# Where the second rounding of weights is kept: out of PSUM in one half of up, into PSUM in the early projection

## The chip, the cores and the metric

The kernel runs on one core of a Trainium2 chip. The metric is device time in microseconds (us): the median of three runs. One more execution was profiled; its trace gives the rows below.

## The reference

One layer of a streaming encoder on 512 tokens of width 2048, in float32. A vector c conditions it: `mod = silu(c) @ ada_w + ada_b` gives six rows of 2048 (shift, scale and gate of the mixing half, and of the FFN half).

```
h = rms_norm(x, mix_pre_g) * (1 + sc_m) + sh_m
y = token_mixers(h, w_in, ...)          # one input projection, four mixers, one output projection
x = x + gt_m * rms_norm(y, mix_post_g)
h = rms_norm(x, ffn_pre_g) * (1 + sc_f) + sh_f
a, gt = split(h @ w_up)                 # 2048 x 11008
a = causal_dwconv(a, conv_w) + conv_b   # 3 taps along time
y = (gelu(a) * gt) @ w_down             # 5504 x 2048
x = x + gt_f * rms_norm(y, ffn_post_g)
```

## The kernel before

Every large product is made from two fp32r numbers per operand. `hi` is the operand rounded by a ScalarE copy, `lo` is the rest, made by VectorE as operand minus `hi`, and three matmuls (hi x hi, lo x hi, hi x lo) are summed in PSUM. So each 128 x 512 piece of weights costs a ScalarE copy and a VectorE subtraction. `split` does this for the projections, `dsplit` for the FFN. With `shadow`, `dsplit` makes the rounding twice, once into SBUF (`hi`, for the matmuls) and once into a PSUM bank (`sh`), and VectorE subtracts `sh`. A list, `SHADOW = (0, 1, 2, 3)`, says in which steps of a block.

PSUM has eight banks here: four of the tag `acc` and four of the tag `mx`. Shadows, transposes and small results all take theirs from `mx`.

*Early projection.* The 16 k tiles of h are finished one after another, since each needs its part of `mod`: a matrix-vector product (`gemv_unit`), of which VectorE and GpSimd each sum a half of the units (ScalarE scales GpSimd's half), `join` adds the two, and a matmul with ones turns the row into columns (`mod_cols`, or `first_half` for the first two tiles). Meanwhile the projection columns that are needed first go through the k tiles that exist, in six steps (`KSTEPS`: four of two k tiles, two of four). `fm_group` and `tm_group` make their weights with `wunit`; partial sums are added in SBUF by `ev_early_fm` (L586) and `ev_early_tm` (L598). `x_norm` makes the row of 1/rms of x (`rB`): ScalarE squares 16 tiles, VectorE adds them up.

*Up and down.* `fast_block` makes a block of products with seven steps (`STEPS`) instead of eight; in each step, for each of four weight pieces, two output tiles get three matmuls each. GpSimd makes the differences of weights that the later steps use (L1461, L1464, L1466, L1468; each after the `lo` of the piece that it overwrites). Up runs 20 blocks, ten in each of two halves `p`. In the second half each block's results are complete: its eight 512-column tiles are transposed (`cT`, 32 transposes, two `mx` banks for each of four feature tiles) and go through `glu`: ScalarE, VectorE twice, ScalarE, VectorE once. GpSimd sums the results for down (`put_sums`). Then the next block follows. Down runs ten blocks with the same `fast_block`.

The order of the instructions on each engine is not written out: a planner takes the program's order as priority and what it expects to be ready.

Of the kernel before, what the change touches and what calls it, by code (L numbers as in the profile page):

```python
# [11 lines left out]
F32R = mybir.dt.float32r  # L12
AF = mybir.ActivationFunctionType
# [236 lines left out]
def trunk_kernel(ctx: ExitStack, tc: tile.TileContext, a: dict, out: bass.AP):  # L250
# [33 lines left out]
    def tt_(s="t"):  # L284
        return tp.tile([P, 512], F32, tag="t", name=nm(s))
# [53 lines left out]
        return r, sd  # L339


    def wunit(src, nk, w, own=True):

        raw = wraw() if own else araw()
        nc.sync.dma_start(out=raw[:, :nk * w], in_=src[:, :nk * w])
        step = max(1, 512 // w)
        out_ = []
        for j in range(0, nk, step):
            m = min(step, nk - j) * w
            hi = wp.tile([P, 512], F32R, tag="hi", name=nm("hi"))  # L350
            lo = wp.tile([P, 512], F32R, tag="lo", name=nm("lo"))
            split(raw[:, j * w:j * w + m], hi[:, :m], lo[:, :m])
            out_ += [(hi[:, i * w:(i + 1) * w], lo[:, i * w:(i + 1) * w]) for i in range(min(step, nk - j))]
        return out_

# [3 lines left out]
    def araw():  # L359
        return gp.tile([P, UW], F32, tag="ada", name=nm("ada"), bufs=NADA)  # L360

    def split(src, hi, lo, eng=None):
        S.activation(hi, src, AF.Copy)  # L363
        (eng or V).tensor_tensor(lo, src, hi, ALU.subtract)  # L364

# [29 lines left out]
            return gp.tile([P, 512], dt, tag="ga", name=nm(s), bufs=NGA)  # L395
        return mt(s, dt=dt)

    def gemv_unit(accs, eng, uidx, i, half=None):
        w = 512 if half is None else 256
        if half is None:  # L400
            raw = araw()
            nc.sync.dma_start(out=raw, in_=a["ada"][uidx])
        else:
            raw = mt("ada")
            nc.sync.dma_start(out=v2(raw), in_=v2(a["ada"][uidx])[:, :, half * 256:(half + 1) * 256])
        for j in range(2):
            c1 = cond[:, 2 * i + j:2 * i + j + 1]
            src = raw[:, j * w:(j + 1) * w]
            if eng not in accs:
                accs[eng] = galloc("ga")[:, :w]  # L410
                if eng is V:
                    V.tensor_scalar(accs[eng], src, c1, None, ALU.mult)
                else:
                    S.activation(accs[eng], src, AF.Copy, scale=c1)
            elif eng is V:
                V.scalar_tensor_tensor(accs[eng], src, c1, accs[eng], ALU.mult, ALU.add)  # L416
            else:
                S.activation(src, src, AF.Copy, scale=c1)  # L418
                G.tensor_tensor(accs[eng], accs[eng], src, ALU.add)  # L419

    def join(accs):
        ts = list(accs.values())
        if len(ts) == 2:
            V.tensor_tensor(ts[0], ts[0], ts[1], ALU.add)
        return ts[0]

    def mod_cols(ga, bs1, bsh, g, c):

# [15 lines left out]
        nc.sync.dma_start(out=xT[kt], in_=a["xT"][kt])  # L444

    def x_norm():
        ss = gp.tile([P, 512], F32, name="rB")
        s2 = galloc("ss")
        warm = st(1)
        S.activation(warm, tc0[:, 0:1], AF.Square)  # L450
        S.activation(warm, warm, AF.Sqrt)
        for kt in range(KT):
            a_ = (ss, s2)[kt % 2]
            sq = tt_("sq") if kt > 1 else a_
            S.activation(sq, xT[kt], AF.Square)
            if kt > 1:
                V.tensor_tensor(a_, a_, sq, ALU.add)
        V.tensor_tensor(ss, ss, s2, ALU.add)
        ps = mx("xss")
        for tt in range(NTT):  # L460
            TE.matmul(ps[:, tt:tt + 1], ss[:, tt * P:(tt + 1) * P], ones[:, 0:1], start=True, stop=True)
        r, _ = rstd(ps[:, 0:NTT], D, "rx")
        V.tensor_tensor(v4(ss), rep(ident, 4), bc3(r, P), ALU.mult)
        ps = mx("xrB")
        TE.matmul(ps, ones, ss, start=True, stop=True)
        S.activation(ss, ps, AF.Copy)
        return ss

    rB = x_norm()
# [17 lines left out]
    def first_half(kt):  # L487

        accs = {}
        for i in range(8):  # L490
            gemv_unit(accs, (G if i in HV else V), gada[0][i], i, kt)
        h_ = xn(kt)
        ga = join(accs)
        ps = mx("gps")
        for j in range(2):
            TE.matmul(ps[:, j:j + 1], ga[:, j * P:(j + 1) * P], ones[:, 0:1], start=True, stop=True)
        ca, cb = (cp.tile([P, 1], F32, name=nm("ca")) for _ in range(2))
        sl = slice(kt, kt + 1)
        V.scalar_tensor_tensor(ca, ps[:, 0:1], bsc1[:, sl], cv("preg")[:, sl], ALU.add, ALU.mult)
        V.tensor_tensor(cb, ps[:, 1:2], cv("bsh")[:, sl], ALU.add)  # L500
        make_h(kt, ca, cb, h_)

    def mod_units(c):

        accs = {}
        for i in range(8):
            yield lambda i=i: gemv_unit(accs, (G, V, G, V, G, V, G, V)[i], gada[c][i], i)

        def fin():
            ca, cb = mod_cols(join(accs), bsc1, cv("bsh"), cv("preg"), c)  # L510
            for j in range(2):
                make_h(2 * c + j, ca[:, j:j + 1], cb[:, j:j + 1])

        yield fin
# [10 lines left out]
    def fm_group(g, evict, ws=None):  # L525
        _, keys, ks, step, us = g
        n = len(keys)
        if len(us) == 1:
            (ui, (uk, uc)) = us[0]
            if ws is None:  # L530
                ws = wunit(a["w_in"][ui], len(uk), len(uc))
            for t in range(n):
                p_ = acc()
                o = slice(t * P, (t + 1) * P)
                for j, kt in enumerate(uk):
                    mm3(p_, ws[j][0][:, o], ws[j][1][:, o], hh[kt], hl[kt], j == 0, j == len(uk) - 1)
                evict(keys[t], p_, step)
            return
        ps = None
        for n_, (ui, (uk, uc)) in enumerate(us):  # L540
            ws = wunit(a["w_in"][ui], len(uk), len(uc), n_ % 2 == 0)
            between()
            if ps is None:
                ps = [acc() for t in range(n)]
            for j, kt in enumerate(uk):
                for t in range(n):
                    o = slice(t * P, (t + 1) * P)
                    mm3(ps[t], ws[j][0][:, o], ws[j][1][:, o], hh[kt], hl[kt], kt == ks[0], kt == ks[-1])
        for t in range(n):
            evict(keys[t], ps[t], step)  # L550
# [889 lines left out]
        eng.tensor_tensor(l_, src, h_, ALU.subtract)  # L1440
        return h_, l_

    def fast_block(A, src, units, bank, evict, after):
        b = []
        for j in range(NP):
            d = {}
            for x, (k0, k1) in enumerate((("B11", "B12"), ("B22", "B21"))):
                raw = draw()
                nc.sync.dma_start(out=raw, in_=src[units[2 * j + x]])
                d[k0], d[k1] = raw[:, 0:512], raw[:, 512:]  # L1450
            b.append(d)
        banks = {}
        for i, (ch, fresh, _, key, half, co) in enumerate(STEPS):
            if fresh:
                banks[ch] = [bank(ch) for _ in range(2)]
            ah, al = A[i]
            for j in range(NP):
                d = b[j]
                wh, wl = dsplit(d[key], V, i in SHADOW)
                if i == 0:  # L1460
                    G.tensor_tensor(d["B11"], d["B12"], d["B11"], ALU.subtract)  # L1461
                    d["T1"] = d["B11"]
                    d["T2"] = t2()
                    G.tensor_tensor(d["T2"], d["B22"], d["T1"], ALU.subtract)  # L1464
                if i == 1:
                    G.tensor_tensor(d["B12"], d["B22"], d["B12"], ALU.subtract)  # L1466
                    d["T3"] = d["B12"]
                    G.tensor_tensor(d["B21"], d["B21"], d["T2"], ALU.subtract)  # L1468
                    d["T4"] = d["B21"]
                for t in range(2):  # L1470
                    sl = slice(j * 256 + t * P, j * 256 + (t + 1) * P)
                    ps = banks[ch][t]
                    st_, sp_ = fresh and j == 0, j == NP - 1
                    TE.matmul(ps, ah[:, sl], wh, start=st_, stop=False, skip_group_check=True)  # L1474
                    TE.matmul(ps, ah[:, sl], wl, start=False, stop=False, skip_group_check=True)  # L1475
                    TE.matmul(ps, al[:, sl], wh, start=False, stop=sp_, skip_group_check=True)  # L1476
            for t in range(2):
                evict(2 * half + t, co, banks[ch][t])
            after(i)
# [39 lines left out]
    for p in range(2):  # L1519
        for n in range(NB):  # L1520
# [15 lines left out]
            def after(i, p=p, n=n, c=c):  # L1536
# [7 lines left out]
                if n == NB - 1:  # L1544
# [1 line left out]

            u0 = (p * NB + n) * NP * 2
            fast_block(A, a["w_up"], gup[1][u0:u0 + 2 * NP], acc,
                       lambda tt, co, ps, c=c: add_to(c, tt, co, ps, ctile), after)
            if p:  # L1550
                for m in range(0, 4, 2):
                    f0 = 4 * n + m
# [109 lines left out]
HV = (1, 4)  # L1662
FS0 = (1, 4, 4, 3, 3)
NA0 = 2


# [14 lines left out]
```

## Time and profile before

| | |
|---|---|
| median of 3 runs | 2443.0 us (2441.74 to 2444.22) |
| profiled execution | 2445.28 us, its span 2443.5 us |
| TensorE matmuls | busy 2229.2 us, 91% of the span |
| VectorE | busy 1765.2 us, 72% |
| ScalarE | busy 1429.3 us, 58% |
| GpSimd | busy 1103.9 us, 45% |
| mean granted clock of TensorE | 0.968 of full speed |

The span runs from the first to the last instruction; the rest of the execution's time lies around it. Busy time of TensorE is that of pipelined matmuls, so its share alone doesn't say whether it could go faster. PE is TensorE (PEld its weight load), DVE is VectorE, ACT is ScalarE, POOL is GpSimd; L1440 is line 1440 of the kernel.

### The profile page before, as it was taken

Reading aid. Unit: us, or ns where it says so; the run is one execution under the profiler, and the core shown is the slowest. Engines: PE = TensorE matmul, PEld = TensorE weight load, DVE = VectorE, ACT = ScalarE, POOL = GpSimd, SP = SyncE. Lnnn points to the kernel's source line nnn. Section 1 sums busy time; section 2 is a strip of 40 time slices with the busy share of each in tenths; the row PEclk is TensorE's granted clock in tenths of the full one; section 3 lists DMA queues with packets and bytes.
Section 4 is the critical chain, followed back from the end, with each engine's and each line's share of the span. In section 5 each row is a group of like instructions: output and inputs, shape, how many; then the busy total and the mean of one; then the engine's idle time right before and its main releaser. Section 6 shows DMA issues by size and latency. Waiting matters only on the chain. (4 is left out here: it accounts for less than half of the span.)

```text
span 2443.5 us, 31280 instructions
## 1 busy us (share of the span) xinstructions
PE 2229.2 (91%) x9854; PEld 1755.3 (72%) x9854; DVE 1765.2 (72%) x2671; ACT 1429.3 (58%) x2578; POOL 1103.9 (45%) x847
## 2 busy tenths in 40 slices
PE   4989999989998998999999999988888989999998
PEld 2767877777776786777777777767667767777776
DVE  7898669977878646766655767776776776777767
ACT  5544355354466544576676775655565667667653
POOL 4673023233333201485544555544455556565553
PEclk9989999999999999999999999999999999999999
DMA  7667555677787744778745465444444454334433
GB/s 266 251 219 250 172 171 177 199 234 261 262 294 269 258 144 150 264 250 300 247 157 170 153 242 174 164 172 164 147 172 164 138 190 155 137 140 162 148 108 147
DMA packets 206030, 479.19 MB, mean 196 GB/s; under 512 B 32660, under 2 KB 74148, under 8 KB 205864
## 3 DMA queue, kind: packets, MB, share of 16 engines
q1 hardware_dynamic: 199032, 476.14, 55.9%
q10 hardware_dynamic: 6832, 1.06, 0.2%
q8 instruction: 78, 1.28, 0.2%
q14 instruction: 88, 0.72, 0.1%
HBM read 398.46 MB, written 78.67 MB: 195 GB/s over the span
## 5 line engine op out<-in xcount | busy, mean ns | idle before, releaser
L419 POOL TENSOR_TENSOR ga<-ga,ada 128x512 f32<-128x512 f32 (+1 forms) x167 | 247.4, 1482 | 436.2 <-ACT ada L418 417.8
L1475 PE MATMUL X<-lo,ah 128*128 128x512 f32 x960 | 392.7, 409 | 33.9 <-DVE lo L1437 29.9
L1474 PE MATMUL X<-hi,ah 128*128 128x512 f32 x960 | 388.2, 407 | 28.2 <-DVE c L1486 18.2
L1476 PE MATMUL X<-hi,al 128*128 128x512 f32 x960 | 389.4, 406 | 0.0
L1440 DVE TENSOR_TENSOR lo<-raw,hi 128x512 fp32r<-128x512 f32 x360 | 284.9, 838 | 73.8 <-ACT hi L1439 73.7
L1461 POOL TENSOR_TENSOR raw<-raw 128x512 f32<-128x512 f32 x120 | 164.0, 1370 | 294.6 <-ACT hi L1436 160.6
L1474 PE MATMUL Z<-hi,ah 128*128 128x512 f32 x720 | 284.0, 397 | 9.3 <-ACT c L1484 8.2
L1475 PE MATMUL Z<-lo,ah 128*128 128x512 f32 x720 | 284.8, 396 | 1.5 <-DVE lo L1440 1.5
L1476 PE MATMUL Z<-hi,al 128*128 128x512 f32 x720 | 284.8, 396 | 0.0
L1437 DVE TENSOR_TENSOR lo<-raw,sh 128x512 fp32r<-128x512 f32 x360 | 233.5, 682 | 47.2 <-ACT sh L1435 28.2
L1435 ACT ACTIVATE sh<-raw 128x512 fp32r<-128x512 f32 x360 | 205.4, 586 | 102.5 <-DMA raw<-w_dn 61.8
L1436 ACT ACTIVATE hi<-raw 128x512 fp32r<-128x512 f32 x360 | 221.1, 623 | 75.6 <-PE Z L1476 29.1
L1439 ACT ACTIVATE hi<-raw 128x512 fp32r<-128x512 f32 x360 | 207.9, 623 | 74.7 <-DVE lo L1440 30.3
L1475 PEld LDWEIGHTS X<-lo,ah 128*128 128x128 f32 x960 | 187.3, 195 | 82.3 <-DVE lo L1437 34.1
L364 DVE TENSOR_TENSOR lo<-raw,hi 128x512 fp32r<-128x512 f32 (+1 forms) x218 | 184.3, 856 | 82.0 <-ACT hi L363 81.2
L1474 PEld LDWEIGHTS X<-hi,ah 128*128 128x128 f32 x960 | 185.3, 194 | 81.1 <-ACT hi L1439 10.5
L367 PE MATMUL acc<-hh,hi 128*128 128x512 f32 x544 | 225.7, 418 | 14.1 <-ACT lt L744 7.0
L369 PE MATMUL acc<-hh,lo 128*128 128x512 f32 x544 | 224.3, 414 | 8.4 <-DVE lo L364 8.2
L368 PE MATMUL acc<-hl,hi 128*128 128x512 f32 x544 | 223.9, 412 | 2.0 <-POOL hl L480 2.0
L1476 PEld LDWEIGHTS X<-hi,al 128*128 128x128 f32 x960 | 187.7, 196 | 44.4
L363 ACT ACTIVATE hi<-raw 128x512 fp32r<-128x512 f32 (+1 forms) x218 | 130.6, 613 | 151.2 <-PE y L555 51.4
L416 DVE SCALAR_TENSOR_TENSOR ga<-ada,cond,ga 128x512 f32<-128x512 f32 (+1 forms) x183 | 180.3, 985 | 12.0 <-DMA ada<-ada 10.1
(376 smaller groups left out, 4615.5 us busy)
## 6 DMA issues: line engine op xcount, KB each, us to landing
ada<-ada SPq DMA_DIRECT2D x184, 512.0 KB, 4.5
raw<-w_up SPq DMA_DIRECT2D x172, 512.0 KB, 5.6
raw<-w_dn SPq DMA_DIRECT2D x86, 512.0 KB, 5.0
raw<-w_in SPq DMA_DIRECT2D x56, 512.0 KB, 4.5
partd<-c SPq DMA_DIRECT2D x80, 256.0 KB, 3.4
c<-partd SPq DMA_DIRECT2D x80, 256.0 KB, 3.7
actd<-q SPq DMA_DIRECT2D x40, 512.0 KB, 4.4
ar<-actd SPq DMA_DIRECT2D x35, 512.0 KB, 3.2
```

The source lines that it names most:

```text
L367: TE.matmul(o, sh, mh, start=first, stop=False)
L368: TE.matmul(o, sh, ml, start=False, stop=False)
L369: TE.matmul(o, sl, mh, start=False, stop=last)
L419: G.tensor_tensor(accs[eng], accs[eng], src, ALU.add)
L1435: S.activation(sh, src, AF.Copy)
L1436: S.activation(h_, src, AF.Copy)
L1437: V.tensor_tensor(l_, src, sh, ALU.subtract)
L1439: S.activation(h_, src, AF.Copy)
L1440: eng.tensor_tensor(l_, src, h_, ALU.subtract)
L1474: TE.matmul(ps, ah[:, sl], wh, start=st_, stop=False, skip_group_check=True)
L1475: TE.matmul(ps, ah[:, sl], wl, start=False, stop=False, skip_group_check=True)
L1476: TE.matmul(ps, al[:, sl], wh, start=False, stop=sp_, skip_group_check=True)
```

## The change

In the half of up with transposes no step makes a second rounding into PSUM any more. In the early projection three things change: the weights of the column groups with one unit get the second rounding from step 1 on; VectorE's sums of the matrix-vector product live in a PSUM bank instead of SBUF; and the squares of x are summed over the k tiles and partitions by matmuls with ones into one PSUM bank (of each four tiles two are first added on VectorE), after which square root and reciprocal run on the whole 128 x 512 tile.

```diff
-            split(raw[:, j * w:j * w + m], hi[:, :m], lo[:, :m])
+            split(raw[:, j * w:j * w + m], hi[:, :m], lo[:, :m], None, shadow)
...
-    def split(src, hi, lo, eng=None):
+    def split(src, hi, lo, eng=None, shadow=False):
+
+        if shadow:
+            sh = pp.tile([P, 512], F32R, tag="mx", name=nm("sh"))[:, :src.shape[1]]
+            S.activation(sh, src, AF.Copy)
+            S.activation(hi, src, AF.Copy)
+            V.tensor_tensor(lo, src, sh, ALU.subtract)
+            return
...
-                accs[eng] = galloc("ga")[:, :w]
+                if eng is V and bank is not None:
+                    accs[eng] = bank[:, :w]
+                else:
+                    accs[eng] = galloc("ga")[:, :w]
...
-        ts = list(accs.values())
-        if len(ts) == 2:
-            V.tensor_tensor(ts[0], ts[0], ts[1], ALU.add)
-        return ts[0]
+        if len(accs) == 2:
+            V.tensor_tensor(accs[G], accs[G], accs[V], ALU.add)
+        return accs[G]
...
+        ps = mx("xss")
+        odd = None
         for kt in range(KT):
-            a_ = (ss, s2)[kt % 2]
-            sq = tt_("sq") if kt > 1 else a_
+            sq = mt("sq")
             S.activation(sq, xT[kt], AF.Square)
-            if kt > 1:
-                V.tensor_tensor(a_, a_, sq, ALU.add)
-        V.tensor_tensor(ss, ss, s2, ALU.add)
...
+            if kt % 4 == 0:
+                odd = sq
+                continue
+            if kt % 4 == 1:
+                V.tensor_tensor(sq, odd, sq, ALU.add)
+            TE.matmul(ps, ones, sq, start=kt == 1, stop=kt == KT - 1)
+        S.activation(ss, ps, AF.Sqrt, bias=epst, scale=1.0 / D)
+        V.reciprocal(ss, ss)
         return ss
...
+        bk = mx("ga")
         for i in range(8):
-            gemv_unit(accs, (G if i in HV else V), gada[0][i], i, kt)
+            gemv_unit(accs, (G if i in HV else V), gada[0][i], i, kt, bk)
         h_ = xn(kt)
         ga = join(accs)
-        ps = mx("gps")
+        ps = bk[:, 256:258]
...
-        accs = {}
+        accs, bk = {}, []
+
+        def unit(i):
+            if i == 1:
+                bk.append(mx("ga"))
+            gemv_unit(accs, (G, V)[i % 2], gada[c][i], i, None, bk[0] if bk else None)
...
-                ws = wunit(a["w_in"][ui], len(uk), len(uc))
+                ws = wunit(a["w_in"][ui], len(uk), len(uc), True, SH_IN and step > 0)
...
-    def fast_block(A, src, units, bank, evict, after):
+    def fast_block(A, src, units, bank, evict, after, shadow=SHADOW):
...
-                wh, wl = dsplit(d[key], V, i in SHADOW)
+                wh, wl = dsplit(d[key], V, i in shadow)
...
-                       lambda tt, co, ps, c=c: add_to(c, tt, co, ps, ctile), after)
+                       lambda tt, co, ps, c=c: add_to(c, tt, co, ps, ctile), after, (SHADOW, ())[p])
...
+SH_IN = True
```

## Rows read from the trace of the kernel before

**Rows 1.** Busy time (instructions) by stretch: up without, and with transposes.

```profile
core 0: us, PE busy (x) PEld busy (x) DVE busy (x) ACT busy (x) POOL busy (x), PEclk, DMA share, GB/s
...
1300.00:1400.00 100.00, 99.31 (x425) 79.42 (x424) 60.86 (x86) 72.67 (x134) 48.92 (x38) 1.00 0.44 150
...
1700.00:1800.00 100.00, 87.82 (x384) 69.04 (x383) 69.33 (x103) 58.82 (x102) 51.58 (x48) 0.95 0.46 157
```

**Rows 2.** Waits of TensorE, 1540 to 1990 us: total us, times, longest.

```profile
PE X L1475 <- DVE lo L1437: 24.1, 9, 2.7
```

**Rows 3.** Timeline of TensorE at a block's end: start, us, instruction, idle before.

```profile
1554.30 2.04 PE L1559 MATMUL cT<-cst,c 128*128 128x128 f32 x16
...
1558.55 1.28 PE L1559 MATMUL cT<-cst,c 128*128 128x128 f32 x8 [1.27 <-DVE fa L1360]
...
1564.78 0.51 PE L1475 MATMUL X<-lo,ah 128*128 128x512 f32 x1 [2.73 <-DVE lo L1437]
...
1566.16 0.63 PE L1475 MATMUL X<-lo,ah 128*128 128x512 f32 x1
...
1569.69 0.40 PE L1475 MATMUL X<-lo,ah 128*128 128x512 f32 x1
```

**Rows 4.** Timeline of VectorE over that block and the next one's start.

```profile
1553.80 1.39 DVE L1486 TENSOR_TENSOR c<-c,X 128x512 f32<-128x512 f32 x2 [4.20 <-PE X L1476]
...
1584.21 4.32 DVE L1440 TENSOR_TENSOR lo<-raw,hi 128x512 fp32r<-128x512 f32 x3
...
1605.63 1.39 DVE L1486 TENSOR_TENSOR c<-c,X 128x512 f32<-128x512 f32 x2 [4.21 <-PE X L1476]
```

**Rows 5.** Groups of VectorE, 1540 to 1990 us: busy us, mean ns.

```profile
L1440 DVE TENSOR_TENSOR lo<-raw,hi 128x512 fp32r<-128x512 f32 x102 | 85.8, 893 | 0.5 <-ACT hi L1439 0.4
...
L1437 DVE TENSOR_TENSOR lo<-raw,sh 128x512 fp32r<-128x512 f32 x104 | 65.8, 682 | 4.4 <-ACT sh L1435 4.4
...
L1486 DVE TENSOR_TENSOR c<-c,X 128x512 f32<-128x512 f32 x68 | 45.1, 683 | 55.5 <-PE X L1476 55.3
...
L1359 DVE SCALAR_TENSOR_TENSOR fa<-cT,colp,fa 128x511 f32<-128x511 f32 x36 | 26.1, 746 | 9.1 <-ACT fa L1358 9.1
```

**Rows 6.** One line over the whole span: duration ns, least, median, most.

```profile
L1440 DVE TENSOR_TENSOR lo<-raw,hi x360: 676/684/3464, 1065.1 to 2392.0; 128x512 fp32r<-128x512 f32 x180
```

**Rows 7.** Busy time by stretch, early projection, columns as in rows 1.

```profile
160.00:185.00 25.00, 21.05 (x81) 16.02 (x81) 22.15 (x26) 11.51 (x18) 20.41 (x14) 0.80 0.58 213
...
210.00:235.00 25.00, 25.00 (x130) 21.11 (x129) 18.24 (x26) 10.77 (x18) 10.03 (x7) 1.00 0.65 234
```

**Rows 8.** Timeline of GpSimd after the boundary: the first difference.

```profile
1564.81 1.29 POOL L1461 TENSOR_TENSOR raw<-raw 128x512 f32<-128x512 f32 x1 [0.43 <-DVE lo L1437]
```

**Rows 9.** Timeline of the first 60 us.

```profile
7.97 0.69 DVE L457 TENSOR_TENSOR rB<-rB,sq 128x512 f32<-128x512 f32 x1 [2.92 <-ACT sq L455]
...
21.97 2.07 PE L465 MATMUL xrB<-rB,ones 128*128 128x512 f32 x2 [1.60 <-DVE rB L463]
24.08 0.60 ACT L466 ACTIVATE rB<-xrB 128x512 f32<-128x512 f32 x1 [2.56 <-PE xrB L465]
...
34.13 0.81 ACT L477 ACTIVATE hh<-xn,ca,ca 128x512 fp32r<-128x512 f32 x1 [0.88 <-DVE ca L500]
```

**Rows 10.** The narrow evictions of the early projection: durations, first and last start.

```profile
L598 DVE TENSOR_TENSOR cvb<-cvb,acc x20: 414/418/426, 103.6 to 289.2; 128x264 f32<-128x264 f32 x20
```

**Rows 11.** Groups of VectorE, 60 to 120 us.

```profile
L416 DVE SCALAR_TENSOR_TENSOR ga<-ada,cond,ga 128x512 f32<-128x512 f32 x17 | 20.6, 1212 | 0.2
L364 DVE TENSOR_TENSOR lo<-raw,hi 128x512 fp32r<-128x512 f32 x16 | 16.5, 1034 | 2.2 <-ACT hi L363 2.1
```

**Rows 12.** Groups of VectorE, 120 to 200 us.

```profile
L416 DVE SCALAR_TENSOR_TENSOR ga<-ada,cond,ga 128x512 f32<-128x512 f32 x22 | 24.7, 1122 | 0.1
L364 DVE TENSOR_TENSOR lo<-raw,hi 128x512 fp32r<-128x512 f32 x18 | 23.3, 1294 | 0.0
```

**Rows 13.** Reciprocals of 4 and of 16 columns: duration ns.

```profile
L338 DVE RECIPROCAL rx<-rxd x1: 179/179/179, 20.8 to 20.8; 128x4 f32<-128x4 f32 x1
...
L789 DVE RECIPROCAL pz<-pz x1: 253/253/253, 291.8 to 291.8; 128x16 f32<-128x16 f32 x1
```

More of the change, by code (lines that the diff above doesn't have):

```diff
@@ L339, in rstd, with wunit @@
         return r, sd
-    def wunit(src, nk, w, own=True):
+    def wunit(src, nk, w, own=True, shadow=False):
         raw = wraw() if own else araw()
@@ L396, in galloc, with gemv_unit @@
         return mt(s, dt=dt)
-    def gemv_unit(accs, eng, uidx, i, half=None):
+    def gemv_unit(accs, eng, uidx, i, half=None, bank=None):
         w = 512 if half is None else 256
@@ L447, in x_norm @@
         ss = gp.tile([P, 512], F32, name="rB")
-        s2 = galloc("ss")
         warm = st(1)
@@ L451, in x_norm @@
         S.activation(warm, warm, AF.Sqrt)
+        ps = mx("xss")
+        odd = None
         for kt in range(KT):
-            a_ = (ss, s2)[kt % 2]
-            sq = tt_("sq") if kt > 1 else a_
+            sq = mt("sq")
             S.activation(sq, xT[kt], AF.Square)
-            if kt > 1:
-                V.tensor_tensor(a_, a_, sq, ALU.add)
-        V.tensor_tensor(ss, ss, s2, ALU.add)
[L459 to L466, printed above, removed]
+            if kt % 4 == 0:
[6 more added lines that the diff above has]
+        V.reciprocal(ss, ss)
         return ss
@@ L503, in mod_units @@
     def mod_units(c):
-        accs = {}
+        accs, bk = {}, []
[3 more added lines that the diff above has]
+            gemv_unit(accs, (G, V)[i % 2], gada[c][i], i, None, bk[0] if bk else None)
         for i in range(8):
-            yield lambda i=i: gemv_unit(accs, (G, V, G, V, G, V, G, V)[i], gada[c][i], i)
+            yield lambda i=i: unit(i)
         def fin():
```

## The prediction

> **What bounds the kernel now.** I read the busy time by stretch first, then TensorE's waits in the stretches where it isn't full, then single boundaries in the timeline. Where the half of up without transposes runs, TensorE is at its end: 425 matmuls in 100 us, 0.235 us each, 99% busy. In the half with transposes it is busy for 88 of 100 us, and neither VectorE (69) nor ScalarE (59) nor GpSimd (52) is full [rows 1]. So there something is late once in a while. The largest wait of that half is a matmul of the first step of a block that waits for its `lo` [rows 2].
>
> The timeline of one boundary shows why. A block's last step ends, 16 transposes run from 1554.30, then TensorE idles in small pieces until 1564.78: 1.27 us for `fa` of the GLU, 2.73 us for `lo` [rows 3]. In those 8.4 us from 1556.34 it issues 16 more transposes (0.127 us each, 2.04/16) and, from the order of the code, four matmuls that need only `hi`, 3.0 us in all; 5.4 us are idle. After it the matmuls last 0.63 instead of 0.40 us for some 4 us: the lower of the clock's two levels, and the granted clock of that half is 0.95 [rows 1, 3]. The cause is PSUM: the tag `mx` has four banks; the GLU of a tile holds two until its last VectorE operation, and a shadow of the next block wants one too. The block's period is 1605.63 - 1553.80 = 51.8 us [rows 4]. TensorE's own work in it is 7 x 4 x 2 x 3 = 168 matmuls at 0.235 and 32 transposes at 0.127: 39.5 + 4.1 = 43.6 us. So 8.2 us a block are lost. There are ten blocks; nine of them are followed by a block that the change alters, the tenth by the first of down, which keeps its shadows.
>
> The early projection is the other place. Its code has 16 x 48 = 768 matmuls of 512 columns and 16 x 12 = 192 of 264 columns: 768 x 0.235 + 192 x 0.12 (scaled by columns, my estimate) = 204 us. It runs from the end of the first `hh` at 34.9 to the last eviction at 289.2 [rows 9, 10], 254 us: 50 us over. In the stretch of 160 to 185 us it has 81 matmuls where the full stretch of 210 to 235 has 130 (the narrow ones among them), a granted clock of 0.80, VectorE busy for 22 of 25 us and GpSimd for 20 [rows 7].
>
> **Part A, up without shadows.** Removed: 16 `sh` copies of ScalarE per block, and with them 16 claims on `mx`. ScalarE was not the bound, so its time is worth nothing. The `hi` of steps 0 and 1 of the next block are written while steps 5 and 6 of the old one still run, as now; but `lo` then needs no bank, and VectorE is idle for 4.20 us just before the boundary [rows 4]. With 8 pairs of `hi`, `lo` two steps (11 us of matmuls) can lie ready when the transposes come, so they cover the chain of the GLU. If that is all, the 8.2 us go: 9 x 8.2 = 74 us.
>
> The price is on VectorE. A `lo` whose second operand is in PSUM takes 0.682 us, always; one with both in SBUF has a mean of 0.893 us in this stretch [rows 5], with a median of 0.684 and a maximum of 3.464 [rows 6]. Where GpSimd works back to back, three took 4.32 us, 1.44 each [rows 4]. Per block VectorE has 28 `lo`, 14 evictions at 0.68 and 12 GLU operations at 0.75: 19.1 + 9.5 + 9.0 = 37.6 us without any contention. GpSimd has 16 differences at 1.29 [rows 8] = 21 us and 8 half-wide sums, and it makes them just while the 16 `lo` of steps 0 to 3 are wanted. For what each of these 16 then pays I have: nothing; +0.35 us (1.034, early stage, 60 to 120 us); +0.61 us (1.294, 120 to 200 us) [rows 11, 12]; +0.76 (the 1.44 above); +2.78 for one that waits like the maximum. I take +0.61: the stretch where VectorE mixes the same kinds of operations and GpSimd is as full. The other 12 keep their +0.21. VectorE then needs 37.6 + 9.8 + 2.5 = 49.9 us per block and becomes the bound in place of the bank: 51.8 - 49.9 = 1.9 us, times 9: **17 us less**. Bounds: 74 us less (TensorE's floor); at +0.76 a block takes 52.3 us, 4 us more over the nine; and if 4 of the 16 wait like the maximum, 37.6 + 4 x 2.78 + 12 x 0.61 + 2.5 = 58.5 us, 60 us more.
>
> The rows show the asymmetry without its reason. The Trainium skill, page "SBUF — State Buffer", section "Who interferes with whom", gives a rule that speaks against this part: VectorE with two SBUF inputs and GpSimd reading SBUF share one port as an exclusive lock, and the later one waits for the whole instruction, while an operand in PSUM keeps VectorE out of it. The trace agrees with both halves (0.682 against up to 3.464). By that rule all of the 16 could wait for one GpSimd operation of 1.29 us [rows 8]: 37.6 + 16 x 1.29 + 2.5 = 60.7 us a block, 80 more over nine, where the rows that I take give 17 less. The same mechanism, priced from the rows of this kernel, is the third rival.
>
> **Part B, the early stage.** Three edits.
>
> PSUM accumulators: the sums of `gemv_unit` on VectorE read and write a bank. The nearest row for the new form is the GLU's operation with one operand in PSUM, 0.746 us [rows 5], against 1.122 (22 of them, 120 to 200 us) and 1.212 (17, 60 to 120 us): 8.3 + 7.9 us less for VectorE. Shadows for the early weights from step 1: the `lo` go from 1.294 (18) and 1.034 (16) to 0.682: 11.0 + 5.6 us less [rows 11, 12]. In sum 33 us of VectorE between 60 and 200 us. Against it stand 56 more ScalarE copies (24 in steps 1 to 3, 32 in steps 4 and 5) at 0.60 us (a copy between SBUF and PSUM [rows 9]) = 34 us, spread over some 200 us in which ScalarE is busy for 11.5 of 25 us [rows 7]: covered. If the cover goes, the scaling of GpSimd's half of the gemv and `hh` queue behind them on ScalarE. The four banks of `mx` now hold one or two accumulators, `gps` and shadows; while step 0 holds three of them, the sums of the next column block wait.
>
> TensorE lost 50 us here, VectorE gets back 33. I take 20, since VectorE is full only in part of the stage and waits for the ada loads and for clock stay; bounds: nothing (ScalarE or the banks take its place) and 40.
>
> Square sums on TensorE: 15 VectorE additions of 0.69 [rows 9] become 4, and 12 matmuls with fp32 operands of 512 columns come in. One such takes 2.07 us at the lower clock [rows 9], so 12 take 24.8, or half of it at the upper level: 12.4. The first can start at about 8.5 us (the first addition of today begins at 7.97), so the sum is there between 20.9 and 33.3 us; I take the middle, 27.1. Then a square root (0.60, as the copy that it replaces) and a reciprocal of 512 columns, which no row shows: 4 columns take 0.179, 16 take 0.253 us [rows 13]; this slope gives 3.3 us as an estimate, an ordinary VectorE operation of this width 0.69. So `rB` comes at about 31 us instead of 24.7. But `rB` isn't what is last today: `hh` starts at 34.13 [rows 9] behind the join of the gemv on VectorE, which now has 7 us less of additions ahead of it. I count **2 us less** (from 8 less to 8 more).
>
> **Sum.** 17 + 20 + 2 = 39 us less. The profiled execution has 2445.3 us (span 2443.5 and 1.8 around it): 2406; against the median of 2443.0 that is 2404.
>
> **The rivals.**
> 1. *TensorE's floor in up.* GpSimd's differences can start as soon as each `lo` of step 0 is done, ahead of the boundary, and VectorE is idle there; if collisions fall into idle time, the whole 8.2 us go. 74 + 22 = 96 us less: 2347. Against it: VectorE would have to do 37.6 us plus collisions in 43.6.
> 2. *The stall only changes its name.* VectorE reaches the GLU late because its `lo` stand behind GpSimd, and the transposes, in TensorE's order, wait for `fa` and `q` as long as they did for the banks. Up gains nothing, the early stage 22: 2421.
> 3. *Slower.* GpSimd's chain of differences holds VectorE for several operations, as for the maximum of 3.464 us; 4 such waits a block make 58.5 us of it: 60 more, less 22: 2481. It decides for slower from a block of 54.3 us on, where up loses the 22 us that the early stage gains. For it: all of the 16 `lo` stand in GpSimd's busy half. Against: VectorE has 12 us idle per block now.
> 4. *Nothing anywhere.* ScalarE's copies and the banks of `mx` hold the early stage where it is, and up is as in 2: 2443.
>
> **How the numbers follow.** The forecast has 0.42 (own range 2380 to 2425), rival 1 0.15, rival 2 0.20, rival 3 0.13, rival 4 0.10. 0.2% of 2443 is 4.9 us, about what a measurement of this kernel can tell from no change. Forecast, 1 and 2 are faster: 0.77, with 0.02 of rival 4: 0.79; rival 3 is slower, 0.13, with 0.01 of rival 4: 0.14; the rest, 0.07, within. The range goes from 2350 (most of rival 1 on its inner side) to 2450 (beyond rival 4), and leaves out rival 3 and the outer part of 1.
>
> **What would show it.** Up: no wait of a matmul for `lo` or of `cT` for `fa` over 1 us, a period of about 50 us, a mean `lo` of about 1.2 us, VectorE over 90% busy. If the period is near 44, rival 1; if `cT` still waits, rival 2. Early: `ga` at about 0.75 us, the last eviction of `cvb` near 267 instead of 289.2, ScalarE under 70%. The start: `hh` near 32 us, the reciprocal's duration, the clock of the square sums. The prediction is wrong if a bank of `mx` is the longest wait of the early stage, or if VectorE is under 80% busy in up with a period still over 51 us.

## The result, and the profile after

The changed kernel takes 2381.2 us (median of 4 runs, 2380.07 to 2384.11), the kernel before 2442.4 beside it: a ratio of 0.9755, 95% interval 0.9737 to 0.9773. That is 61 us less, where 39 were forecast. The profiled span is 2378.2 us instead of 2443.5, the mean granted clock 0.973.

Where the time came from is read off two lines whose start times mark the ends of the two stages: the narrow evictions of the early projection, and the transposes of up. Their durations in ns (least, median, most), first and last start; the transposes before, then both after:

```profile
L1559 PE MATMUL cT<-cst,c x320: 270/273/478, 1502.2 to 1981.6; 128*128 128x128 f32 x160
...
L612 DVE TENSOR_TENSOR cvb<-cvb,acc x20: 420/422/430, 96.4 to 276.7; 128x264 f32<-128x264 f32 x20
...
L1573 PE MATMUL cT<-cst,c x320: 270/273/476, 1485.9 to 1911.9; 128*128 128x128 f32 x160
```

The last narrow eviction starts 12.5 us earlier than in [rows 10]. The transposes of the kernel before ran from 1502.2 to 1981.6, 479.4 us; now it is 426.0, 53.4 less. From block to block they start 52.1 us apart before and 46.0 after, the mean of eight periods; the ninth, ahead of the first block of down, is 53.3 and 48.1. So a block takes 6.1 us less.

The two profiled executions differ by 65.3 us, more than the medians, since the one before is slower than the four timed here and the one after the fastest of its kernel. Of the 65.3, 12.5 come up to the last narrow eviction, 3.8 between it and the first transpose, 53.4 in up, and 4.4 are lost again behind it. The 3.8 and the 4.4 show nothing by themselves: behind the last transposes come between 461.3 and 466.8 us in the eleven traces whose program there is that of before (466.1 in psum_only below, whose up is unchanged), and between the narrow evictions and the transposes 1206.8 to 1213.6 us in all fourteen.

Up with transposes, busy time by stretch after, columns as in [rows 1]:

```profile
1600.00:1700.00 100.00, 95.97 (x444) 77.33 (x443) 93.63 (x121) 50.23 (x80) 66.00 (x49) 1.00 0.54 191
1700.00:1800.00 100.00, 94.84 (x428) 77.15 (x427) 91.30 (x117) 48.20 (x77) 63.69 (x48) 0.97 0.56 199
```

VectorE went from 69 to over 90 of 100 us and TensorE from 88 to 95 or 96. The wait of [rows 2], nine times for `lo`, is gone. TensorE's longest left over from 1490 to 1900 us (us in all, times, longest):

```profile
PE cT L1573 <- DVE c L1500: 18.4, 8, 3.2
```

A transpose now waits for the last evictions of its own block (L1500: VectorE adds a finished bank, `X` or `Z`, to the block's result `c`), 2.3 us each time. The timelines of one boundary show why, TensorE first (start, us, instruction, idle before):

```profile
1669.94 0.93 PE L1573 MATMUL cT<-cst,c 128*128 128x128 f32 x7
1672.88 1.25 PE L1573 MATMUL cT<-cst,c 128*128 128x128 f32 x9 [2.01 <-DVE c L1500]
...
1676.77 0.63 PE L1573 MATMUL cT<-cst,c 128*128 128x128 f32 x4
```

VectorE at the same time, and 14 us before it:

```profile
1652.22 2.48 DVE L1454 TENSOR_TENSOR lo<-raw,hi 128x512 fp32r<-128x512 f32 x4
...
1666.46 5.77 DVE L1454 TENSOR_TENSOR lo<-raw,hi 128x512 fp32r<-128x512 f32 x4
1672.15 1.27 DVE L1500 TENSOR_TENSOR c<-c,X 128x512 f32<-128x512 f32 x2
```

And GpSimd:

```profile
1661.79 1.29 POOL L1475 TENSOR_TENSOR raw<-raw 128x512 f32<-128x512 f32 x1 [11.84 <-DVE lo L1454]
...
1666.46 1.84 POOL L1475 TENSOR_TENSOR raw<-raw 128x512 f32<-128x512 f32 x1
1668.38 1.63 POOL L1478 TENSOR_TENSOR t<-raw,raw 128x512 f32<-128x512 f32 x1
1669.97 1.71 POOL L1480 TENSOR_TENSOR raw<-raw,raw 128x512 f32<-128x512 f32 x1
```

The `lo` of the next block's first steps no longer wait for a bank, so they are made before the boundary, and so are GpSimd's differences that follow each of them. The last matmuls of the block end at 1670, but the evictions stand on VectorE behind four `lo` that take 5.77 us, because GpSimd works through three differences meanwhile. The same four `lo` took 2.48 us where GpSimd was idle. After that wait the transposes (x4, 0.63 us) stand among matmuls without a gap; in [rows 3] TensorE stood still there for `fa` and `lo`.

This wait and the clock after it are what a period of 46.0 us has above TensorE's own time. Two single periods, columns as before:

```profile
1624.90:1669.90 45.00, 42.98 (x201) 34.66 (x200) 42.75 (x55) 22.82 (x36) 32.53 (x25) 1.00 0.51 187
1715.00:1762.50 47.50, 44.34 (x201) 36.24 (x200) 43.85 (x56) 22.64 (x36) 31.56 (x24) 0.96 0.52 177
```

Four of the first eight periods take 45.0 us, with a wait of 2.0 us; without GpSimd's differences (no_diff, below) a period takes 42.8. Two take 46.4, with the same wait but a granted clock of 0.96, and two 47.5, with a wait of 3.2 us and that clock: matmuls behind the wait last 0.63 instead of 0.40 us for a while, the lower of the two levels.

Groups of VectorE from 1490 to 1900 us (busy us, mean ns, idle before):

```profile
L1454 DVE TENSOR_TENSOR lo<-raw,hi 128x512 fp32r<-128x512 f32 x209 | 199.0, 993 | 20.2 <-ACT hi L1453 20.2
...
L1454 DVE TENSOR_TENSOR lo<-t,hi 128x512 fp32r<-128x512 f32 x36 | 39.6, 1119 | 0.0
```

The boundary from up to down is a comparison inside the same run: down's first block still makes its shadows. TensorE there:

```profile
1902.00 2.04 PE L1573 MATMUL cT<-cst,c 128*128 128x128 f32 x16
...
1908.33 1.28 PE L1573 MATMUL cT<-cst,c 128*128 128x128 f32 x8 [3.37 <-DVE fa L1374]
...
1914.62 0.79 PE L1489 MATMUL X<-lo,ah 128*128 128x512 f32 x1 [2.33 <-DVE lo L1451]
```

The stall of [rows 3] is there once, with both of its waits; from 1490 to 1900 us TensorE has neither. What becomes of this boundary without the shadows is shown by down_first below.

The early projection, 60 to 120 us of VectorE, columns as in [rows 11]:

```profile
L368 DVE TENSOR_TENSOR lo<-raw,sh 128x512 fp32r<-128x512 f32 x16 | 10.7, 682 | 6.2 <-ACT sh L366 6.1
...
L426 DVE SCALAR_TENSOR_TENSOR ga<-ada,cond,ga 128x512 f32<-128x512 f32 x14 | 10.5, 749 | 0.0
```

Busy time by stretch there:

```profile
60.00:85.00 25.00, 25.00 (x124) 20.87 (x123) 15.75 (x27) 21.31 (x40) 14.46 (x12) 1.00 0.69 240
...
135.00:160.00 25.00, 15.22 (x63) 12.23 (x61) 15.81 (x29) 13.54 (x24) 15.61 (x13) 0.78 0.74 257
160.00:185.00 25.00, 24.93 (x106) 20.17 (x107) 20.23 (x31) 15.52 (x26) 12.62 (x11) 0.88 0.67 236
```

Both operations cost what the prediction put down, and in the stretch of [rows 7], 160 to 185 us, TensorE is now busy throughout, at a granted clock of 0.88. But 135 to 160 us isn't, and VectorE, ScalarE and GpSimd all have nine or more of the 25 us free there. Waits from 130 to 165 us (us in all, times, longest):

```profile
PE acc L376 <- DVE lo L368: 7.0, 3, 3.8
...
DVE lo L368 <- ACT sh L366: 6.5, 3, 2.7
...
ACT ga L424 <- DMA ada<-ada: 7.9, 2, 4.5
ACT ada L428 <- DMA ada<-ada: 6.1, 2, 3.5
```

ScalarE waits for loads of `ada`, the `lo` wait for ScalarE, and TensorE waits for the `lo`.

### The profile page after: what moved, and what is told of

Same layout as the page of the kernel before. It is cut to its first block, busy times and chain, and to the rows that moved or that the text cites. A ratio compares the mean times of both kernels' runs of the same rounds, so it can differ in the third digit from the quotient of the medians.

```text
span 2378.2 us, 31052 instructions
## 1 busy us (share of the span) xinstructions
PE 2204.4 (93%) x9868; PEld 1744.9 (73%) x9868; DVE 1783.3 (75%) x2659; ACT 1381.2 (58%) x2473; POOL 1143.5 (48%) x847
## 5 line engine op out<-in xcount | busy, mean ns | idle before, releaser
L1454 DVE TENSOR_TENSOR lo<-raw,hi 128x512 fp32r<-128x512 f32 x480 | 414.1, 904 | 96.9 <-ACT hi L1453 96.7
L429 POOL TENSOR_TENSOR ga<-ga,ada 128x512 f32<-128x512 f32 (+1 forms) x167 | 236.0, 1413 | 454.2 <-ACT ada L428 433.3
L1453 ACT ACTIVATE hi<-raw 128x512 fp32r<-128x512 f32 x480 | 288.0, 627 | 189.4 <-PE X L1490 72.5
L1475 POOL TENSOR_TENSOR raw<-raw 128x512 f32<-128x512 f32 x120 | 172.9, 1443 | 410.9 <-ACT hi L1450 178.1
L1488 PE MATMUL Z<-hi,ah 128*128 128x512 f32 x720 | 286.1, 398 | 15.2 <-DVE c L1500 5.9
L1449 ACT ACTIVATE sh<-raw 128x512 fp32r<-128x512 f32 x240 | 138.6, 588 | 98.5 <-DMA raw<-w_dn 57.8
L1451 DVE TENSOR_TENSOR lo<-raw,sh 128x512 fp32r<-128x512 f32 x240 | 157.7, 681 | 45.3 <-ACT sh L1449 23.5
L371 DVE TENSOR_TENSOR lo<-raw,hi 128x512 fp32r<-128x512 f32 (+1 forms) x162 | 124.8, 784 | 70.7 <-ACT hi L370 70.1
L1488 PEld LDWEIGHTS Z<-hi,ah 128*128 128x128 f32 x720 | 136.1, 189 | 53.2 <-ACT c L1498 8.7
L1478 POOL TENSOR_TENSOR t<-raw,raw 128x512 f32<-128x512 f32 x120 | 172.0, 1437 | 5.3
L1480 POOL TENSOR_TENSOR raw<-raw,raw 128x512 f32<-128x512 f32 x120 | 165.9, 1384 | 0.3
```

Source lines behind the costliest of these rows:

```text
L1453: S.activation(h_, src, AF.Copy)
```

## The experiments

Every run was timed beside the kernel before on the same chip, and the ratios are against that. The theory was: in up, the shadows' claim on `mx` made the stall, and what remains is the collision of VectorE and GpSimd; the early part adds to it.

**Each half by itself.** The kernel before with the change of up alone (a_only), and the changed kernel with the old steps in up (b_only).

```diff
-                       lambda tt, co, ps, c=c: add_to(c, tt, co, ps, ctile), after)
+                       lambda tt, co, ps, c=c: add_to(c, tt, co, ps, ctile), after, (SHADOW, ())[p])
```

> The kernel before with the change in up alone (no shadows in the half with transposes; the early stage as before). If the two parts are independent, the distance between first and last transposes, 479.4 us before and 426.0 after, is again 426 and the time is 2443 - 54 + 4 = 2393 us (the 4 us are lost behind up in the changed kernel, too). Rival: the blocks of up are shorter only because the planner ordered them anew together with the early stage: a period of 48 us or more, 2410 or more.

> The kernel before with the early part of the change alone (all three edits), up with its shadows as before. If the parts add, it is the distance between the changed kernel and the one with up alone: 2381 - 2394.5 = 13 us less than before, about 2429; the last eviction of the early stage near 277 us as in the changed kernel (289.2 before). Rival: the early gain is only passed on because up has room; then under 5 us less.

Measured: a_only 2394.5 us, 0.9806 (0.9785 to 0.9826), 47 less; b_only 2430.2 us, 0.9945 (0.9928 to 0.9962), 12 less. The transposes of a_only:

```profile
L1573 PE MATMUL cT<-cst,c x320: 270/273/473, 1501.9 to 1926.1; 128*128 128x128 f32 x160
```

424.2 us, as in the changed kernel; the starts are again 46.0 us apart. 47 + 12 = 59 of the 61: within the intervals the two halves add.

**Is it the bank or ScalarE's time?** As a_only, but steps 0 to 3 make the second rounding again, into the SBUF tile that then takes `lo`. ScalarE's work is that of before; no bank is claimed.

```diff
+        if shadow is None:
+            S.activation(l_, src, AF.Copy)
+            S.activation(h_, src, AF.Copy)
+            V.tensor_tensor(l_, src, l_, ALU.subtract)
+            return h_, l_
...
-                wh, wl = dsplit(d[key], V, i in shadow)
+                wh, wl = dsplit(d[key], V, (None if i in SHADOW else False) if shadow == () else i in shadow)
```

> As a_only, but in the 16 places of a block where the shadow was, ScalarE still makes the second rounding, into the SBUF tile of lo itself, and VectorE subtracts it there in place. So ScalarE has the work of before, no bank of mx is claimed, and VectorE reads both operands from SBUF. Theory (the bank is what made the stall): as a_only within 8 us, about 2393 to 2401. Rival (ScalarE's time made it): a period of 50 us or more and 2430 or more.

Measured: 2388.9 us, 0.9787 (0.9761 to 0.9812); transposes from 1498.0 to 1921.0, 423 us. ScalarE was at 69 of 100 us:

```profile
1600.00:1700.00 100.00, 95.87 (x441) 77.59 (x439) 92.43 (x122) 68.90 (x119) 70.77 (x54) 0.98 0.50 177
```

All of the gain of up is there with ScalarE's copies in place. The bank made the stall.

**What GpSimd's differences cost.** The changed kernel without the 16 differences in that half.

```diff
-                if i == 0:
+                if i == 0 and shadow == ():
+                    d["T1"], d["T2"], d["T3"], d["T4"] = d["B11"], d["B22"], d["B12"], d["B21"]
+                elif i == 0:
...
-                if i == 1:
+                if i == 1 and shadow != ():
```

> The changed kernel without GpSimd's 16 differences of weights per block in the half of up with transposes (the later steps take plain weights, so the output is not the reference's). Theory (VectorE is the bound of a block, by waiting for GpSimd's operations): the mean lo there falls from 0.99 to about 0.75 us, VectorE has 39 us per block instead of 44, the period goes from 46.0 to TensorE's 44 and the time to about 2363 us. Rival (the order on TensorE, transposes behind the GLU, holds the block): the period stays at 46 and the time at 2381.

Measured: 2340.5 us, 0.9585 (0.9551 to 0.962). The transposes span 393.1 us, and from block to block they start 42.8 us apart, each of the eight times. One such period:

```profile
1531.20:1574.00 42.80, 42.80 (x201) 34.76 (x200) 34.96 (x55) 22.68 (x36) 6.65 (x8) 1.00 0.65 221
```

And the subtractions, and one stretch of VectorE's timeline at a boundary:

```profile
L1454 DVE TENSOR_TENSOR lo<-raw,hi 128x512 fp32r<-128x512 f32 x193 | 136.2, 721 | 50.2 <-ACT hi L1453 50.2
```

```profile
1658.99 0.69 DVE L1454 TENSOR_TENSOR lo<-raw,hi 128x512 fp32r<-128x512 f32 x1 [0.70 <-ACT hi L1453]
1659.60 1.28 DVE L1502 TENSOR_TENSOR c<-c,X 128x512 f32<-128x512 f32 x2
```

The transposes begin at 1659.54, the last evictions at 1659.60 with no `lo` ahead of them, and the wait is gone; a `lo` takes 0.72 us. TensorE is at its floor, 42.8 us. It moved further than the theory asked, which had 44 us a period and 18 us in all: the transposes span 33 us less than in the changed kernel, and the median is 41 less. The run takes out the collisions and also the dependence of the later steps on GpSimd; since in the changed kernel from 1490 to 1900 us TensorE and VectorE have no wait of note for GpSimd, and ScalarE's `hi` wait for it 9.5 us in all, I put most of it down to the collisions. The two are not taken apart by a run.

**Shadows only where no GLU holds the banks.** The changed kernel with shadows in steps 2 and 3.

```diff
-                       lambda tt, co, ps, c=c: add_to(c, tt, co, ps, ctile), after, (SHADOW, ())[p])
+                       lambda tt, co, ps, c=c: add_to(c, tt, co, ps, ctile), after, (SHADOW, (2, 3))[p])
```

> The changed kernel with shadows again in steps 2 and 3 of the blocks with transposes, none in steps 0 and 1. Theory: the bank matters only for the pieces that are wanted while the GLU holds mx, which are those of steps 0 and 1; shadows in steps 2 and 3 spare VectorE half of its collisions (8 lo at 0.3 to 0.5 us), the period falls from 46.0 to about 44.5 and the time to about 2368. Rival: any shadow in a block brings the wait for a bank back: a period of 50 or more, 2415 or more.

Measured: 2375.0 us, 0.9723 (0.9694 to 0.9751); transposes over 420.3 us, 5.7 less than in the changed kernel, about half of what the theory gave. By the time alone the gain isn't clear, since the intervals of the two ratios overlap; the transposes bear it out (420.3, and 420.5 and 422.0 in best1 and best2 with the same steps, against 424.2 to 426.0 in the three versions without any second rounding there). The stall did not come back: shadows in steps 2 and 3 are harmless, so those of steps 0 and 1, which no run has alone, made it. VectorE fell to 86 of 100 us, yet TensorE stayed at 96. And VectorE at a block's end:

```profile
1650.00:1750.00 100.00, 95.97 (x446) 77.61 (x445) 85.79 (x120) 57.58 (x96) 58.24 (x49) 1.00 0.58 209
```

```profile
1845.76 5.77 DVE L1454 TENSOR_TENSOR lo<-raw,hi 128x512 fp32r<-128x512 f32 x4
1851.46 1.27 DVE L1500 TENSOR_TENSOR c<-c,X 128x512 f32<-128x512 f32 x2
```

The wait of `cT` for the last evictions is still there (12.1 us in 6 waits from 1550 to 1850), and so are four `lo` of 5.77 us just ahead of them. Six of the first eight periods take 44.9 us, against 45.0 in the changed kernel with 3.4 us more of VectorE's work; what went are the waits of 3.2 us and some of the spells at the lower clock. So it isn't VectorE's sum that sets the period now but the place of the colliding `lo`.

**The edits of the early stage one at a time.** Each alone on the kernel before: accumulators in PSUM; shadows in `wunit`; squares on TensorE.

```diff
-            gemv_unit(accs, (G if i in HV else V), gada[0][i], i, kt)
+            gemv_unit(accs, (G if i in HV else V), gada[0][i], i, kt, bk)
...
-                ws = wunit(a["w_in"][ui], len(uk), len(uc))
+                ws = wunit(a["w_in"][ui], len(uk), len(uc), True, SH_IN and step > 0)
...
+            TE.matmul(ps, ones, sq, start=kt == 1, stop=kt == KT - 1)
```

> Only VectorE's sums of the matrix-vector product in PSUM. Theory (VectorE, delayed by GpSimd, was the bound from 85 to 160 us): the sums go from 1.12 to 1.21 us to 0.75, some 16 us of VectorE fall away and the last eviction comes 5 to 8 us earlier, about 2436. Rival (either edit alone frees VectorE enough, the next wait is the ada loads): nearly all of the 12.5 us, about 2430.

> Only the second rounding for the early weights. Theory: 17 us of VectorE fall away, 34 us come to ScalarE, the last eviction comes 4 to 7 us earlier, about 2437. Rivals: as for the sums alone (nearly all of the 12.5 us), or nothing, since ScalarE's copies stand ahead of the h tiles in its queue.

> Only the square sums on TensorE, with square root and reciprocal of the whole tile. Theory: the first h is 0.7 us earlier in the changed kernel because the join of the matrix-vector product, which waits for the ada loads, is last, not the sums: within 3 us of 2443. Rival: the 7 us of VectorE's additions are worth their time: 5 us or more less.

Measured: 2429.3 us, 0.9935 (0.9915 to 0.9955); 2430.2 us, 0.9952 (0.9934 to 0.9969); 2448.8 us, 1.0029 (1.0017 to 1.0041). So 12.5 less, 11.6 less and 7.0 more; together (b_only) 11.5 less. For the first two the rival came true (that nearly all of the 12.5 us come), for the third neither theory nor rival. Either of the first two gives nearly all, and the third is a loss alone. The times don't yet say whether they add: the three alone sum to 17 less, and the interval of b_only goes from 9 to 18. The last narrow eviction does say it, 289.2 us before [rows 10]; with the accumulators alone, the second roundings alone, and all three (b_only):

```profile
L615 DVE TENSOR_TENSOR cvb<-cvb,acc x20: 415/420/430, 94.8 to 270.7; 128x264 f32<-128x264 f32 x20
...
L612 DVE TENSOR_TENSOR cvb<-cvb,acc x20: 416/423/430, 100.9 to 278.4; 128x264 f32<-128x264 f32 x20
...
L612 DVE TENSOR_TENSOR cvb<-cvb,acc x20: 416/423/430, 97.6 to 275.5; 128x264 f32<-128x264 f32 x20
```

Alone they come 18.5 and 10.8 us earlier, the squares 0.3, together 13.7. The accumulators alone do best, 6 us ahead of the changed kernel. A stretch of psum_only:

```profile
135.00:160.00 25.00, 21.20 (x103) 16.07 (x101) 23.85 (x41) 12.34 (x21) 14.42 (x12) 1.00 0.63 232
```

In the same stretch the three versions with second roundings have TensorE busy for 15.2 to 16.6 us (the changed kernel, shin_only, b_only). There the `lo` wait for ScalarE's copies, and ScalarE for `ada`; that this is the reason is argued from the waits, and no run shows it.

What the squares cost at the start shows in the timeline of sq_only:

```profile
22.11 3.35 DVE L473 RECIPROCAL rB<-rB 128x512 f32<-128x512 f32 x1 [1.91 <-ACT rB L472]
...
31.43 5.35 DVE L426 SCALAR_TENSOR_TENSOR ga<-ada,cond,ga 128x256 f32<-128x256 f32 x13
...
38.54 0.81 ACT L484 ACTIVATE hh<-xn,ca,ca 128x512 fp32r<-128x512 f32 x1 [0.36 <-DVE ca L507]
```

The sums of the gemv come after the reciprocal, 13 of them in a row ahead of the join of the first tile, and the first `hh` starts at 38.5 us instead of 34.1 [rows 9]. But the last narrow eviction of this execution starts at 288.9 and the first transpose at 1500.5, no later than before (289.2 and 1502.2). So where the 7 us of the median arise stays open.

**A better version.** Accumulators in PSUM and shadows in steps 2 and 3, without the other two early edits (best1); the same with shadows (2, 3) in down's first block (best2); that with shadows in steps 2 to 6 in up (best3); and the changed kernel with no shadow in down's first block (down_first).

```diff
+                       lambda tt, co, ps, c=c: add_to(c, tt, co, ps, ctile), after, (SHADOW, (2, 3))[p])
...
-SH_IN = True
+SH_IN = False
...
-                       lambda tt, co, ps, c=c: add_to(c, tt, co, ps, ctile), after, (SHADOW, (2, 3))[p])
+                       lambda tt, co, ps, c=c: add_to(c, tt, co, ps, ctile), after, (SHADOW, (2, 3, 4, 5, 6))[p])
...
-                       lambda tt, co, ps, np_=np_: add_to(ya, tt, 2 * np_ + co, ps, ytile), after)
+                       lambda tt, co, ps, np_=np_: add_to(ya, tt, 2 * np_ + co, ps, ytile), after, SHADOW if g or np_ else (2, 3))
```

> The kernel before with VectorE's gemv sums in PSUM and, in the half of up with transposes, shadows in steps 2 and 3 alone; no second rounding and no square sums in the early stage. Theory (what each part gave alone): 2394.5 for up alone, less 12.5 for the sums, less 6 for the shadows in steps 2 and 3: 2376. If what the sums gained at the end of the early stage (18 us there, 12.5 for both other versions) reaches the end, 2370. Rival: without second roundings the early stage is again bound by VectorE once up is no longer the bound: 2385 or more.

> As best1, and the first block of down takes shadows in steps 2 and 3 alone as well. The last transposes are followed by that block; in the changed kernel TensorE idles there for 6 us and runs at the lower clock for some 4 us after it, as at every boundary before. Theory (the bank, again): that stall goes, 6 to 8 us less than best1. Rival: the block waits for its operands, which are loaded from what the last blocks of up store: no change.

> As best2, with shadows in steps 2 to 6 of the blocks with transposes. Theory (VectorE's waits for GpSimd): the 8 half-wide sums of GpSimd per block, each of which holds up one lo of steps 4 to 6 by 0.54 us, cost nothing more: VectorE has 4 us less per block and the period falls by 1 to 2 us, 9 to 18 us less than best2. Rival (bank): shadows of steps 5 and 6 still hold banks when the next transposes want theirs, the period grows: 10 us or more above best2.

> The changed kernel with no shadows in the first block of down. Theory (bank): the stall behind the last transposes goes, 6 to 8 us less than the changed kernel, less what GpSimd's differences now cost VectorE in that one block (2 to 4 us): 2375 to 2379. Rival (operands from up's last stores): 2381.

Measured: best1 2367.6 us, 0.9682 (0.966 to 0.9705): 14 us under the changed kernel, the intervals of the two ratios apart; it is the second value of the theory (2370), not the first (2376). best2 2366.0 us, 0.9691 (0.9668 to 0.9714), and best3 2366.2 us, 0.968 (0.966 to 0.97): no further change that these runs can tell; both theories missed. down_first 2382.2 us, 0.9745 (0.9725 to 0.9766): no change either. In down_first the waits for `fa` and `lo` at the boundary to down went, as the theory said, but one longer wait came behind them. TensorE's, ScalarE's and the DMA queue's (SPq) longest waits from 1915 to 1960 us:

```profile
PE Z L1488 <- ACT c L1498: 8.8, 1, 8.8
...
ACT sh L1449 <- DMA raw<-w_dn: 18.8, 2, 16.0
...
SPq L1307 <- POOL q L1306: 21.1, 2, 18.6
```

In the queue's order the loads of down's weights (from 1942.55 us) stand behind a store that waits until 1938.62 us for GpSimd's sums (`q`), and GpSimd made down's differences, from 1903.55 to 1934 us, ahead of these sums. So the loads come no earlier for the stall being gone: 36.1 us after the block's first transpose, where it was 35.5 in the changed kernel. ScalarE waits 16.0 us for them, and TensorE 8.8 us where `fa` and `lo` had cost 5.7. best2 has the same wait of TensorE with 5.7 us. That stall went with the shadows, too, but the next limit is close behind it: not operands that up stores, as the rival said, but weights whose loads queue behind up's stores. That best3 gave nothing fits what sh23 showed: its periods are 45.4 us as in best1 and best2 (45.3 and 45.5), and the four `lo` of 5.8 us ahead of the evictions are still there; they belong to the first steps, whose shadows made the stall.

## Why the prediction was right, and where it was off

*The diagnosis* held at each point: the bank of `mx` was what was late (sh_in_slot; the boundary to down, and what down_first took from it), ScalarE's time was worth nothing, and with the claim gone the `hi` and `lo` of two steps lie ready and cover the GLU.

*The size of part A* was off: 53 us where 17 were forecast. The step that failed reads "VectorE then needs 37.6 + 9.8 + 2.5 = 49.9 us per block and becomes the bound in place of the bank". Two of its terms were too large. First, it summed durations: 37.6 without any contention and 2.5 for the twelve `lo` is 40.1 us a block, while [rows 1] has VectorE busy for 69.3 of 100 us, 35.9 a period, with that contention in it. Operations of VectorE that follow each other without a wait start 0.60 us apart and last 0.68 (four `lo` in 2.48 us), so 54 operations, if all followed each other so, would take 54 x 0.08 = 4.3 us less than their sum. Second, the price of collisions: with 209 `lo` at 0.993 and 36 at 1.119 the mean is 1.011 us, so a block's 28 take 28.3 us, where the forecast had 19.1 + 9.8 + 2.5 = 31.4. The rate of the early stage was too high for this one. With both, the need is 49.9 - 4.3 - 3.1 = 42.5 us; measured, VectorE was busy for 384.65 us in the nine periods from 1485.9 to 1902.0 us, 42.7 each. That is no more than TensorE's own 42.8 us in no_diff. So VectorE was over 90% busy, as forecast, but its total doesn't set the period (sh23: 86%, and 45.3 us on average). What does is where the collisions fall: a wait of 2.0 to 3.2 us per block at the last evictions, and the lower clock after it in half of the blocks, which make up the 3.2 us between 42.8 and 46.0.

The Trainium skill, page "SBUF — State Buffer", section "Who interferes with whom", says that VectorE and GpSimd hold their shared port as an exclusive lock. That agrees with this trace in direction: 5.77 us for four `lo` beside differences, 2.48 without, and 0.68 with a PSUM operand. The price for which the prediction took this rule, a whole GpSimd operation for each of 16 `lo` (16 x 1.29 + 2.5 = 23.1 us a block), did not come: the mean was 0.33 us above the 0.68, 9.2 us for the 28 `lo` of a block.

*Rival 1*, TensorE's floor, was the right mechanism for what the bank gave, and no_diff reached that floor once the differences were gone: 42.8 us a block, where the prediction had 43.6. *Rival 2* was half seen: a wait of `cT` did take the place of the one removed, for the evictions and not for `fa`, at 2.3 us a block instead of the 8.2 that the prediction put on the whole stall. *Rival 3*, the slower one, did not come: a GpSimd chain stretches four `lo` to 1.44 us each, but GpSimd was busy for 66 of 100 us and most `lo` went free: the median of the 209 is 0.693 us.

*Part B*: 12.5 us at the last narrow eviction and 12 in time (b_only), where 20 + 2 were forecast. The operations cost what was put down (0.749 against 0.746, 0.682 as it stood), but "VectorE gets back 33. I take 20" counted two reliefs of one engine as if each were on the path. With both VectorE is no longer last from 135 to 160 us (15.8 of 25 busy); the loads of `ada` and ScalarE are. With one alone VectorE is still busy for 23.6 to 25 of 25 us from 85 to 160, so why either gives nearly all the time stays open. The "covered" for ScalarE's copies failed in the stretch from 135 to 160 us, where the `lo` wait for `sh`; from 60 to 85 us ScalarE was busy for 21.3 of 25, above the "under 70%", but TensorE was full there. At the start the timeline after shows:

```profile
8.26 12.55 PE L471 MATMUL xss<-sq,ones 128*128 128x512 f32 x24 [8.26 <-DVE sq L470]
...
21.64 3.35 DVE L473 RECIPROCAL rB<-rB 128x512 f32<-128x512 f32 x1 [1.28 <-ACT rB L472]
...
33.43 0.81 ACT L484 ACTIVATE hh<-xn,ca,ca 128x512 fp32r<-128x512 f32 x1 [4.59 <-DVE ca L508]
```

The 12 products (two instructions each in the trace) took 12.55 us, the lower of the two values that were named; the reciprocal 3.35 us, where its slope gave 3.3; `rB` came at 25.0 instead of 31, and `hh` at 33.4 instead of 32. So the start gave 0.7 us and not 2, and the squares by themselves, without the other two edits, cost 7 in the median.

*The sum*: part A gave three times its 17 us and part B half of its 22. That 39 came as near to 61 as it did is luck in so far as the two errors go against each other. The 2381 us lie at the very edge of the forecast's own range (2380 to 2425), toward rival 1; the period, 46.0, is nearer to rival 1's 44 than to the forecast's 50.

## What to carry to other kernels

When several engines each have room and one is late once per block, look for the buffer that is claimed across the boundary, and give up the claim only in the steps where it is contended: here steps 0 and 1, not all four. Before pricing an engine as the next bound, take its rate from the start times of back-to-back operations, and ask where its slow operations stand in its queue, not only how many there are. Edits that relieve the same engine may be worth one gain together, so try them one at a time: one of the three here was a loss, and one alone brought the stage's end forward more than all three. Before lifting a stall, look at what stands next in the queues: at the boundary to down a wait as long was behind it.

## What the runs showed of the hardware

- Successive 128 x 512 float32 operations of VectorE overlap: each lasts 0.68 us, but they start 0.60 us apart.
- VectorE and GpSimd slow each other when VectorE's operands both lie in SBUF: four `lo` went from 2.48 to 5.77 us, and the differences beside them from 1.29 to between 1.63 and 1.84 us.
- A reciprocal of 128 x 512 takes 3.35 us, some five times a subtraction of that size.
